# Four heads at a time in the decay weights of a chunked scan, and a ring of split activations in a pool of its own

## The chip, the cores and the metric

The kernel runs on one core of one Trainium2 chip. The metric is the device time of one execution in microseconds; lower is better. A core has TensorE (PE in the profile, with PEld for its weight loads), VectorE (DVE), ScalarE (ACT), GpSimd (POOL) and SyncE (SP), which issues the DMAs.

## The reference

One inference step of a hybrid backbone with 4 layers, 128 context tokens and 256 latent tokens, model width 1024. Layers 0 and 3 mix tokens by a bidirectional state-space scan (SSD), layer 1 by a short convolution, layer 2 by differential attention. Each is followed by a gated feed-forward network. The part that the change touches is the scan, here cut to its core for one direction (32 heads in 8 groups, chunks of 128 tokens):

```python
acs = jnp.cumsum(dtc * a, axis=2)
decay = jnp.exp(jnp.where(mask, acs[:, :, :, None] - acs[:, :, None], -jnp.inf))
cb = jnp.einsum('bcqgn,bcsgn->bcqsg', cc, bc)
y_diag = jnp.einsum('bcqsgr,bcsgrp->bcqgrp', cb[..., None] * decay * dtc[:, :, None], xf)
...
y = rmsnorm(y.reshape(bsz, L, SSM_D_INNER) * jax.nn.silu(z), norm_g)
return y @ w_out
```

It runs forwards and backwards, and both results are added.

## The kernel before

All 384 tokens are kept as three tiles of 128. Products with weights are made from float32r parts: a weight chunk is split into a high part (ScalarE, L155, `wh`) and a low part (VectorE, L156, `wl`), and three matmuls per block of 128 channels use hh, hl and wh, wl (L340 for channel-major blocks, L380 for the token-major output). The chunks stream from HBM through rings (`ahead`, L143). Modulation units (L187, `modps`) are put between the products by `pace`.

An SSD layer is `ssd` (L506). It opens a layer's pool `pl`, and inside it a core pool for the scan. `ssd_core` (L611) goes over 8 groups of four heads. While the scan of group g runs, the projections of group g + 1 are made (L340, then the convolution at L396 to L400), and the gate of group g (`sz`, L631). `scan` is a generator; its five steps are put between the projections. For each of the 3 chunks, `decay` (L674) builds the weights of the token pairs for the four heads:

- GpSimd: `e` = the backward difference for all four heads, 512 columns (L678), and `w` = C.B masked, times dt, backwards (L679).
- VectorE, once per head on 128 columns: `e` = min(forward difference, `e`) (L682).
- ScalarE: exp of `e` (L683).
- VectorE, once per head: `w` = C.B masked, times dt forwards, plus `w` (L686), then `w` times `e` for all heads (L687).

`e` and `w` share a ring of 4 buffers of 512 columns. For chunks 1 and 2 VectorE also makes `ab` (L693), the weights of the incoming states. The matmuls `yp` (L722) use them. The group ends with y (L741), the gate's product (L637), its square (L642) and the sum of squares `ssq` on GpSimd (L643).

After the groups, `ssq` goes through a matmul (`sps`, L523), and `tm_out` (L351) multiplies y by the output weights (L380): 16 steps of k, each with nine matmuls for a half of the columns. For each k, `prep` (L528) splits y into `yh` (ScalarE, L532) and `yl` (VectorE, L533). These lie in rings of RB = 7 buffers in the layer's pool `pl`.

The order on each engine is not the order of the code: the program is built with a scheduler that places instructions of the whole layer by a timeline of its own, and inserts waits. Buffers of a closed pool are given back tile by tile (`reuse_waits="tile"`), so a tile of a later pool waits for the last user of the space that it covers.

Of the kernel before, what the change touches and what calls it, by code (L numbers as in the profile page):

```python
# [10 lines left out]
F32 = mybir.dt.float32  # L11
F32R = mybir.dt.float32r
# [7 lines left out]
P = 128  # L20
# [24 lines left out]
class Net:  # L45
# [22 lines left out]
    @contextmanager  # L68
    def banked(self, **banks):
        """Five banks of PSUM, by what they are for."""  # L70
        with self.tc.tile_pool(name="ps", bufs=1, space=PSUM, reuse_waits="tile") as ps:
            self.ps, self.banks = ps, banks
            yield
# [46 lines left out]
    def plan(self, l):  # L120
        """The chunks of weights that layer l multiplies with, in their order."""
# [21 lines left out]
    def ahead(self):  # L143
        """Start the loads and the splits of the next chunks."""
# [14 lines left out]
    def weights(self, n):  # L159
        """The next chunk, [128, n], as two float32r parts whose sum it is; those after it are on their way."""  # L160
        self.ahead()
        assert self.wplan[self.wpos][1] == n
        self.wpos += 1
        return self.parts[self.wpos - 1]

# [1 line left out]
    def mod_units(self, l):  # L167
        """Closures that compute layer l's modulation; a unit is a megabyte of w_mod."""
# [56 lines left out]
    def modbuf(self):  # L225
        """A buffer for a unit of w_mod: the standing ones, or one of those that a phase has room for."""
# [15 lines left out]
    def pace(self, phase, n, of):  # L242
        """Modulation beside the products of a phase, n parts of which are done."""
# [15 lines left out]
    def sums(self, src):  # L259
        """Row sums of the squares of half a row, over D."""  # L260
# [5 lines left out]
    def rstd(self, sa, sb, eps=EPS):  # L266
        """(sa + sb + eps) ** -0.5"""
# [11 lines left out]
    def normed(self, t, ss):  # L279
        """The rows of token tile t, normed."""  # L280
# [7 lines left out]
    def turned(self, xn, banks=0):  # L288
        """Channel-major: two banks of [128 channels, 4 blocks, 128 tokens]."""
# [8 lines left out]
    def modulated(self, l, which, t, trs):  # L298
        """h's columns of token tile t, in two float32r parts."""
# [14 lines left out]
    def gated(self, t, hf, acc, gt, parts):  # L314
        """Half a token tile of m: its squares' sum and its product with the gate."""
# [5 lines left out]
    def residual(self, t, parts, eps=EPS):  # L321
        """x += gate * rmsnorm(m) * g for token tile t; the new rows' sums of squares."""
# [8 lines left out]
    def cm_block(self, chunks, nblk, b, m=P, tag="mm"):  # L331
        """[m channels, tokens] of h @ W; chunks: (first kb, number, hi, lo) as [128, kb, nblk, m]."""
# [18 lines left out]
    def tm_out(self, *args, room, **kw):  # L351
        """m = g @ W token-major, both halves, then the residual of each token tile."""
# [40 lines left out]
    def conv(self, src, cw):  # L393
        """Depthwise convolution of three taps along the tokens of both groups."""
# [113 lines left out]
    def ssd(self, l, pl, then):  # L508
# [11 lines left out]
        # eps over the square of the rows' norm factor, which is left out of y  # L520
# [7 lines left out]
        def prep(k):  # L528
            hi = pl.tile([P, T], F32R, tag="yh", name="yh", bufs=RB)
            lo = pl.tile([P, T], F32R, tag="yl", name="yl", bufs=RB)  # L530
            g = dn[:, k // 2, k % 2, 1:2]
            S.activation(hi, y[k], AF.Copy, scale=g)  # L532
            V.scalar_tensor_tensor(lo, y[k], g, hi.bitcast(F32), op0=ALU.mult, op1=ALU.subtract)  # L533
            return hi, lo

        self.tm_out(l, 0, 16, prep, eps=eps, then=then, room=1)

    def steps(self, j, keep, pl, between):
        """Time steps and decays: dt, the cumulated a*dt (token-major, and by rows in DRAM), and what states need."""
# [20 lines left out]
        # log1p(u) = 2 atanh(z), z = u / (2 + u) <= 1/3  # L560
# [17 lines left out]
        # cumulated within a chunk, forwards and backwards: rows of heads  # L578
# [15 lines left out]
        # what is left of a step at its chunk's end (for states), and a whole chunk's decay  # L594
# [16 lines left out]
    def ssd_core(self, l, j, keep, cw, dn, y, ssq):  # L611
# [3 lines left out]
        def convs(g, pr, out, tag="mm"):  # L615
            """Two blocks of channels after their convolution and SiLU, channel-major: (B, C) or (x, x)."""
# [28 lines left out]
        def scan(g, blocks):  # L645
# [11 lines left out]
            # token-major copies  # L657
# [14 lines left out]
            tt = lambda nm: pl.tile([P, 512], F32, tag="e", name=nm, bufs=4)  # L672

            def decay(t):  # L674
                # per head and pair of tokens: C.B, the decay of the direction in which it is one, and dt
                per = lambda a, dr: a[:, t, dr * 32 + 4 * g:dr * 32 + 4 * g + 4, None].to_broadcast([P, 4, P])
                e, w = tt("e"), tt("w")
                GP.tensor_tensor(h4(e), h4(abs_[t][:, 1]), per(acs, 1), op=ALU.subtract)  # L678
                GP.tensor_tensor(h4(w), cb[:, 1, t, None, :].to_broadcast([P, 4, P]), per(dt, 1), op=ALU.mult)  # L679
                for h in range(4):  # L680
                    hs, sl = 4 * g + h, slice(h * P, (h + 1) * P)
                    V.scalar_tensor_tensor(e[:, sl], abs_[t][:, 0, sl], acs[:, t, hs:hs + 1], e[:, sl], op0=ALU.subtract, op1=ALU.min)  # L682
                S.activation(e, e, AF.Exp)  # L683
                for h in range(4):
                    hs, sl = 4 * g + h, slice(h * P, (h + 1) * P)
                    V.scalar_tensor_tensor(w[:, sl], cb[:, 0, t, :], dt[:, t, hs:hs + 1], w[:, sl], op0=ALU.mult, op1=ALU.add)  # L686
# [333 lines left out]
```

## Time and profile before

| what | value |
|---|---|
| median of three runs | 2426.16 us (2422.03 to 2428.34) |
| span of the profiled execution | 2425.7 us, 35610 instructions |
| PE busy | 2298.7 us (95%) |
| DVE busy | 1647.8 us (68%) |
| ACT busy | 1225.8 us (51%) |
| POOL busy | 378.5 us (16%) |
| mean granted TensorE clock | 0.974 |

The page gives the profiled execution's span and no other time of its own; the runs of the first row were timed apart. Busy times are unions of an engine's instructions; the scan stages are about 93 to 390 us (layer 0) and 1790 to 2080 us (layer 3) of the span.

### The profile page before, as it was taken

To read this page: it belongs to the slowest core of one execution; us is meant where nothing else is said; L and a number is where in the kernel's file an instruction comes from. 1 tells how busy PE (TensorE), PEld (TensorE's weight loads), DVE (VectorE), ACT (ScalarE), POOL (GpSimd) and SP (SyncE) were. 2 spreads that over 40 slices of the span, in tenths; PEclk is the share of its full clock that TensorE was granted. 3 is DMA by queue.
4 is the path that set the end of the run, shared out by engine and by line. 5 is a ranking of instruction groups with operands and counts; after the bars stand their busy time and mean duration, and the time that the engine had idled before them with its cause. 6 is when DMAs were issued, how large, how long until landed. Compare 5 with 4: busy or idle time off the path is not lost.

```text
span 2425.7 us, 35610 instructions
## 1 busy us (share of the span) xinstructions
PE 2298.7 (95%) x13132; PEld 2007.5 (83%) x13132; DVE 1647.8 (68%) x2926; ACT 1225.8 (51%) x2031; POOL 378.5 (16%) x546
## 2 busy tenths in 40 slices
PE   6889999899999999999999989999998999989998
PEld 3778887599987978998688758998687888779987
DVE  3789877487755447776654547776669988677765
ACT  3646656454444344444544444445555766554444
POOL 1133330100001001000123330000114344010000
PEclk7989999999999999999999989999999999989999
DMA  7556565543547564335435453345455655423342
GB/s 285 173 164 194 171 202 191 200 137 122 165 120 268 212 215 162 130 122 165 148 116 178 164 205 128 123 131 163 138 171 174 194 160 162 133 97 122 126 146 85
DMA packets 113374, 391.79 MB, mean 162 GB/s; under 512 B 13104, under 2 KB 25520, under 8 KB 100912
## 3 DMA queue, kind: packets, MB, share of 16 engines
q1 hardware_dynamic: 113200, 389.52, 49.1%
q8 instruction: 103, 1.69, 0.3%
q14 instruction: 71, 0.58, 0.1%
HBM read 382.39 MB, written 7.08 MB: 161 GB/s over the span
## 4 chain that ended last, share of the span: by engine, by line
PE 76%; DVE 8%; DMA 3%; issue 2%; ACT 2%; POOL 2%; SPq 0%; POOLq 0%; DVEq 0%; ACTq 0%
PE mm L340 42%; PE mm L380 20%; PE mm L807 5%; PE modps L187 2%; PE yp L380 2%; DVE w L686 2%; DVE e L682 1%; DVE wl L156 1%; PE yp L848 1%; PE yp L722 1%; DMA wm<-in_w_mod 1%; DMA h<-in_state 1%; ACT jk L263 1%; DVE w L687 1%; POOL r L273 1%
## 5 line engine op out<-in xcount | busy, mean ns | idle before, releaser
L340 PE MATMUL mm<-hh,wh 128*128 128x384 f32 (+1 forms) x2352 | 798.0, 341 | 19.1 <-DVE cv L400 13.6
L340 PE MATMUL mm<-hl,wh 128*128 128x384 f32 (+1 forms) x2352 | 796.1, 339 | 0.0
L340 PE MATMUL mm<-hh,wl 128*128 128x384 f32 (+1 forms) x2352 | 792.1, 338 | 0.0
L156 DVE TENSOR_TENSOR wl<-wr,wh 128x1024 fp32r<-128x1024 f32 (+2 forms) x466 | 565.3, 1215 | 262.9 <-ACT wh L155 261.1
L155 ACT ACTIVATE wh<-wr 128x1024 fp32r<-128x1024 f32 (+2 forms) x466 | 483.2, 1039 | 328.0 <-PE mm L340 265.0
L340 PEld LDWEIGHTS mm<-hh,wh 128*128 128x128 f32 (+1 forms) x2352 | 444.3, 189 | 45.6 <-DVE cv L400 20.4
L340 PEld LDWEIGHTS mm<-hl,wh 128*128 128x128 f32 (+1 forms) x2352 | 443.9, 189 | 6.5 <-issue 4.2
L340 PEld LDWEIGHTS mm<-hh,wl 128*128 128x128 f32 (+1 forms) x2352 | 443.6, 189 | 2.6 <-issue 0.7
L396 ACT ACTIVATE cv<-mm,fcw 128x384 f32<-128x384 f32 x176 | 100.1, 571 | 233.2 <-PE mm L340 228.2
L380 PE MATMUL mm<-wh,gh 128*128 128x512 f32 x528 | 208.7, 395 | 0.0
L380 PE MATMUL mm<-wl,gh 128*128 128x512 f32 x528 | 208.6, 395 | 0.0
L380 PE MATMUL mm<-wh,gl 128*128 128x512 f32 x528 | 207.9, 395 | 0.0
L271 POOL TENSOR_SCALAR m<-s 128x1 f32<-128x1 f32 x42 | 17.6, 419 | 1146.7 <-ACT jk L263 1145.8
L398 DVE SCALAR_TENSOR_TENSOR cv<-mm,fcw,cv 128x127 f32<-128x127 f32 x352 | 144.1, 410 | 42.6 <-ACT cv L396 42.6
L405 ACT ACTIVATE gh<-fg 128x384 fp32r<-128x384 f32 x176 | 92.2, 524 | 152.6 <-PE mm L380 151.7
L406 DVE TENSOR_TENSOR gl<-fg,gh 128x384 fp32r<-128x384 f32 x176 | 97.6, 557 | 96.7 <-ACT gh L405 96.0
L400 DVE SCALAR_TENSOR_TENSOR cv<-mm,fcw,cv 128x127 f32<-128x127 f32 x352 | 145.8, 415 | 10.8
L380 PEld LDWEIGHTS mm<-wh,gh 128*128 128x128 f32 x528 | 99.0, 187 | 24.9 <-issue 0.8
L380 PEld LDWEIGHTS mm<-wh,gl 128*128 128x128 f32 x528 | 99.0, 187 | 24.3
L380 PEld LDWEIGHTS mm<-wl,gh 128*128 128x128 f32 x528 | 99.0, 187 | 23.9
L686 DVE SCALAR_TENSOR_TENSOR w<-cb,dt,w 128x128 f32<-128x128 f32 x192 | 94.8, 550 | 3.2 <-POOL w L679 3.2
L187 PE MATMUL modps<-wm,sil 128*32 128x512 f32 x496 | 81.8, 658 | 14.1 <-DMA wm<-in_w_mod 13.2
(223 smaller groups left out, 3206.2 us busy)
## 6 DMA issues: line engine op xcount, KB each, us to landing
wr<-in_ffn_up SPq DMA_DIRECT2D x176, 512.0 KB
wm<-in_w_mod SPq DMA_DIRECT2D x62, 1024.0 KB
wr<-in_ssd_in SPq DMA_DIRECT2D x96, 512.0 KB
wr<-in_ffn_down SPq DMA_DIRECT2D x88, 512.0 KB
wx<-in_w_mod SPq DMA_DIRECT2D x34, 1024.0 KB
ab<-acs SPq DMA_DIRECT2D x48, 512.0 KB
wr<-in_ssd_out SPq DMA_DIRECT2D x32, 512.0 KB
wr<-in_sc_in SPq DMA_DIRECT2D x32, 384.0 KB
```

The source lines that it names most:

```text
L155: self.S.activation(hi[:, :m], raw[:, :m], AF.Copy)
L156: self.V.tensor_tensor(lo[:, :m], raw[:, :m], hi[:, :m].bitcast(F32), op=ALU.subtract)
L187: self.PE.matmul(acc[32 * j:32 * j + 32, :], self.sil[:, kb, :], raws[:, j // 2, (j % 2) * 512:(j % 2 + 1) * 512], start=kb == 0, stop=kb ...
L340: self.PE.matmul(acc[:m], w, h, start=n == 0, stop=n == len(ops) - 1)
L380: self.PE.matmul(acc[t], g[:, o:o + n], w, start=k == 0 and i == 0, stop=k == nk - 1 and i == 2)
L396: self.S.activation(t, src, AF.Copy, scale=cw[:, 1:2])
L398: self.V.scalar_tensor_tensor(t[:, o + 1:o + n], src[:, o:o + n - 1], cw[:, 0:1], t[:, o + 1:o + n], op0=ALU.mult, op1=ALU.add)
L400: self.V.scalar_tensor_tensor(t[:, o:o + n - 1], src[:, o + 1:o + n], cw[:, 2:3], t[:, o:o + n - 1], op0=ALU.mult, op1=ALU.add)
L405: self.S.activation(hi, src, AF.Copy)
L406: self.V.tensor_sub(lo, src, hi.bitcast(F32))
L686: V.scalar_tensor_tensor(w[:, sl], cb[:, 0, t, :], dt[:, t, hs:hs + 1], w[:, sl], op0=ALU.mult, op1=ALU.add)
L807: PE.matmul(acc[t][:, :256], h[k][:, o:o + m], w[:, ws], start=k == 0 and i == 0, stop=k == KB - 1 and i == 2)
```

## The change

In `decay`, the eight VectorE instructions of 128 columns become three of 512 columns with broadcast operands (f, the minimum, the sum). The forward product with dt, which was fused into L686, becomes a GpSimd instruction with an output of its own, `u`. A chunk now takes four buffers of 512 columns, and their ring grows from 4 to 9. The rings of `yh` and `yl` leave the layer's pool for a pool that is opened after the core pool of the scan is closed. Comments and docstrings go as well; line numbers behind L527 shift by one, and inside `decay` differently (the new f is L682, minimum L684, `u` L686, sum L687, product L688 of the new file).

```diff
-        def prep(k):
-            hi = pl.tile([P, T], F32R, tag="yh", name="yh", bufs=RB)
-            lo = pl.tile([P, T], F32R, tag="yl", name="yl", bufs=RB)
...
-        self.tm_out(l, 0, 16, prep, eps=eps, then=then, room=1)
+        with self.tc.tile_pool(name=f"yhl{l}", bufs=1, reuse_waits="tile") as yp:
+            def prep(k):
+                hi = yp.tile([P, T], F32R, tag="yh", name="yh", bufs=RB)
+                lo = yp.tile([P, T], F32R, tag="yl", name="yl", bufs=RB)
...
+            self.tm_out(l, 0, 16, prep, eps=eps, then=then, room=1)
...
-            tt = lambda nm: pl.tile([P, 512], F32, tag="e", name=nm, bufs=4)
+            tt = lambda nm: pl.tile([P, 512], F32, tag="e", name=nm, bufs=9)
...
-                e, w = tt("e"), tt("w")
+                cbd = lambda i: cb[:, i, t, None, :].to_broadcast([P, 4, P])
+                e, f, w, u = tt("e"), tt("f"), tt("w"), tt("u")
                 GP.tensor_tensor(h4(e), h4(abs_[t][:, 1]), per(acs, 1), op=ALU.subtract)
-                GP.tensor_tensor(h4(w), cb[:, 1, t, None, :].to_broadcast([P, 4, P]), per(dt, 1), op=ALU.mult)
-                for h in range(4):
-                    hs, sl = 4 * g + h, slice(h * P, (h + 1) * P)
-                    V.scalar_tensor_tensor(e[:, sl], abs_[t][:, 0, sl], acs[:, t, hs:hs + 1], e[:, sl], op0=ALU.subtract, op1=ALU.min)
+                V.tensor_tensor(h4(f), h4(abs_[t][:, 0]), per(acs, 0), op=ALU.subtract)
+                GP.tensor_tensor(h4(w), cbd(1), per(dt, 1), op=ALU.mult)
+                V.tensor_tensor(e, f, e, op=ALU.min)
                 S.activation(e, e, AF.Exp)
-                for h in range(4):
-                    hs, sl = 4 * g + h, slice(h * P, (h + 1) * P)
-                    V.scalar_tensor_tensor(w[:, sl], cb[:, 0, t, :], dt[:, t, hs:hs + 1], w[:, sl], op0=ALU.mult, op1=ALU.add)
+                GP.tensor_tensor(h4(u), cbd(0), per(dt, 0), op=ALU.mult)
+                V.tensor_tensor(w, w, u, op=ALU.add)
                 V.tensor_tensor(w, w, e, op=ALU.mult)
```

The order on VectorE in the last scan group of layer 0, before, from the masked C.B (`cb`) on:

```order
L670 TENSOR_TENSOR cb<-cbp,trr 128x384 x2
L714 TENSOR_TENSOR s<-sp,s 128x256 x2
L686 SCALAR_TENSOR_TENSOR w<-cb,dt,w 128x128 x4
L682 SCALAR_TENSOR_TENSOR e<-ab,acs,e 128x128 x4
L687 TENSOR_TENSOR w<-w,e 128x512
L156 TENSOR_TENSOR wl<-wr,wh 128x1024
```

and at the same place now:

```order
L671 TENSOR_TENSOR cb<-cbp,trr 128x384 x2
L682 TENSOR_TENSOR f<-ab,acs 128x512
L715 TENSOR_TENSOR s<-sp,s 128x256 x2
L682 TENSOR_TENSOR f<-ab,acs 128x512
L687 TENSOR_TENSOR w<-w,u 128x512
L156 TENSOR_TENSOR wl<-wr,wh 128x1024
L688 TENSOR_TENSOR w<-w,e 128x512
L684 TENSOR_TENSOR e<-f,e 128x512
L694 TENSOR_TENSOR ab<-ab,cv 128x1024
```

The eight short instructions of a chunk are three long ones; the differences f stand ahead of the sums, and the first chunk's minimum has moved to before `cb`.

The order on TensorE at the end of the last projection of layer 0 (L340), before (`sp` is a chunk's state, `yp` the scan's output):

```order
L340 MATMUL mm<-hh_255,wl 128x384
L704 MATMUL sp<-xw,bt 128x256
L187 MATMUL modps<-wm,sil 32x512 x4
L380 MATMUL mm<-wh,yh 128x512
L380 MATMUL mm<-wl,yh 128x512
L380 MATMUL mm<-wh,yl 128x512
```

and now:

```order
L705 MATMUL sp<-xw,bt 128x256
L723 MATMUL yp<-w,xt 64x128 x4
L723 MATMUL yp<-ab,h_3238 64x128 x4
L723 MATMUL yp<-ab,s 64x128 x4
L187 MATMUL modps<-wm,sil 32x512 x4
L723 MATMUL yp<-w,xt 64x128 x4
L723 MATMUL yp<-ab,s 64x128 x4
L723 MATMUL yp<-ab,h_3240 64x128 x4
L201 MATMUL tp<-ident,brow 128x128 x4
L187 MATMUL modps<-wm,sil 32x512 x4
L523 MATMUL sps<-ones_126,ssq 128x1 x3
L380 MATMUL mm<-wh,yh 128x512
```

The output's products, which stood directly behind the projection and between the scan's, stand behind all of `yp` and behind the matmul on `ssq`. The first modulation unit with weights in the output's pool follows 15 of them later.

The order on ScalarE at the end of the scan of layer 0, before (`sq` is the square of the gated y):

```order
L691 ACTIVATE ab<-ab 128x1024
L532 ACTIVATE yh<-y_349,dn 128x384
L532 ACTIVATE yh<-y_350,dn 128x384
L710 ACTIVATE s<-sp 128x256
L155 ACTIVATE wh<-wr 128x1024
```

and now:

```order
L711 ACTIVATE s<-sp 128x256
L643 ACTIVATE sq<-y_356 128x384
L643 ACTIVATE sq<-y_357 128x384
L533 ACTIVATE yh<-y_342,dn 128x384
L533 ACTIVATE yh<-y_343,dn 128x384
L533 ACTIVATE yh<-y_344,dn 128x384
```

Before, `yh` of the eighth y (number 349) is made ahead of the scan's end; now that of the first y (342) comes behind the last squares.

## Rows read from the trace of the kernel before

**Rows 1.** The page: busy times, and the chain that ended last, by engine.
```profile
PE 2298.7 (95%) x13132; PEld 2007.5 (83%) x13132; DVE 1647.8 (68%) x2926; ACT 1225.8 (51%) x2031; POOL 378.5 (16%) x546
...
PE 76%; DVE 8%; DMA 3%; issue 2%; ACT 2%; POOL 2%; SPq 0%; POOLq 0%; DVEq 0%; ACTq 0%
```

**Rows 2.** Busy us by stretch: length, PE, PEld, DVE, ACT, POOL; clock, DMA, GB/s.
```profile
93.00:150.00 57.00, 42.27 (x270) 35.29 (x269) 50.45 (x97) 30.05 (x44) 24.62 (x27) 0.87 0.55 164
150.00:354.00 204.00, 196.57 (x1304) 175.27 (x1303) 169.54 (x315) 128.63 (x181) 73.97 (x75) 0.99 0.59 186
1796.00:1860.00 64.00, 54.59 (x348) 48.40 (x347) 51.48 (x100) 38.52 (x57) 26.15 (x26) 0.97 0.64 178
1860.00:2037.60 177.60, 171.69 (x1195) 156.93 (x1193) 160.87 (x311) 123.55 (x171) 73.31 (x72) 1.00 0.60 184
360.90:379.30 18.40, 18.01 (x124) 12.55 (x124) 18.20 (x33) 12.92 (x17) 3.18 (x2) 1.00 0.50 159
2052.60:2071.80 19.20, 18.58 (x120) 14.18 (x119) 19.09 (x36) 11.19 (x17) 2.25 (x3) 1.00 0.38 102
134.80:145.00 10.20, 5.51 (x40) 3.04 (x37) 10.20 (x24) 2.08 (x4) 3.08 (x3) 0.50 0.60 193
```

**Rows 3.** Waits of PE, 90 to 390 us (first two), 1770 to 2080 us.
```profile
PE yp L722 <- DVE w L687: 9.2, 5, 4.6
PE mm L340 <- DVE cv L400: 7.1, 5, 2.4
...
PE mm L340 <- DVE cv L400: 5.3, 8, 1.5
...
PE yp L722 <- DVE w L687: 4.2, 3, 2.0
```

**Rows 4.** Groups by line and shape: busy us, mean ns, idle before.
```profile
L682 DVE SCALAR_TENSOR_TENSOR e<-ab,acs,e 128x128 f32<-128x128 f32 x192 | 74.7, 442 | 1.3 <-POOL e L678 1.3
L686 DVE SCALAR_TENSOR_TENSOR w<-cb,dt,w 128x128 f32<-128x128 f32 x192 | 94.8, 550 | 3.2 <-POOL w L679 3.2
L687 DVE TENSOR_TENSOR w<-w,e 128x512 f32<-128x512 f32 x48 | 32.6, 678 | 0.1
L693 DVE TENSOR_TENSOR ab<-ab,cv 128x1024 f32<-128x1024 f32 x32 | 40.4, 1262 | 0.2 <-ACT ab L691 0.2
L156 DVE TENSOR_TENSOR wl<-wr,wh 128x1024 fp32r<-128x1024 f32 x432 | 533.9, 1237 | 252.4 <-ACT wh L155 250.7 <-DMA ab<-acs 0.8 <-DMA wr<-in_ssd_out 0.3
L679 POOL TENSOR_TENSOR w<-cb,dt 128x512 f32<-128x512 f32 x48 | 63.8, 1329 | 29.1 <-PE yp L722 15.1 <-DVE w L687 11.0 <-DVE cb L670 2.2
L637 DVE TENSOR_TENSOR y<-y,sz 128x384 f32<-128x384 f32 x32 | 21.9, 693 | 2.4 <-ACT sz L631 2.4
L643 POOL TENSOR_TENSOR ssq<-ssq,sq 128x384 f32<-128x384 f32 x30 | 33.0, 1099 | 62.9 <-ACT sq L642 62.7
```

**Rows 5.** By line and tile: ns min/median/max, first and last start (yh: 93 to 250 us).
```profile
L686 DVE SCALAR_TENSOR_TENSOR w<-cb,dt,w x192: 331/341/1137, 102.8 to 2063.8; 128x128 f32<-128x128 f32 x192
L679 POOL TENSOR_TENSOR w<-cb,dt x48: 1037/1085/3438, 101.7 to 2060.9; 128x512 f32<-128x512 f32 x48
...
L532 ACT ACTIVATE yh<-y,dn x7: 602/604/613, 128.4 to 233.2; 128x384 fp32r<-128x384 f32 x7
```

**Rows 6.** Timeline of DVE, last scan group of layers 0 and 3: start, us.
```profile
355.38 1.02 DVE L670 TENSOR_TENSOR cb<-cbp,trr 128x384 f32<-128x384 f32 x2 [3.60 <-PE cbp L667]
...
373.32 0.69 DVE L687 TENSOR_TENSOR w<-w,e 128x512 f32<-128x512 f32 x1
...
2047.92 1.02 DVE L670 TENSOR_TENSOR cb<-cbp,trr 128x384 f32<-128x384 f32 x2 [2.23 <-PE cbp L667]
```

**Rows 7.** The same stretches for L380 alone (PE and PEld columns only).
```profile
360.90:379.30 18.40, 12.00 (x48) 8.81 (x49) 1.00 0.50 159
2052.60:2071.80 19.20, 14.81 (x56) 10.34 (x57) 1.00 0.38 102
```

**Rows 8.** The chain in order of time, end of the scan of layer 0.
```profile
373.06 2.77 PE yp L722 x48
```

More of the change, by code (lines that the diff above doesn't have):

```diff
@@ L526, in ssd @@
         eps = [ep[:, t:t + 1] for t in range(NT)]
-        def prep(k):
-            hi = pl.tile([P, T], F32R, tag="yh", name="yh", bufs=RB)
-            lo = pl.tile([P, T], F32R, tag="yl", name="yl", bufs=RB)
[L531 to L534, printed above, removed]
-        self.tm_out(l, 0, 16, prep, eps=eps, then=then, room=1)
+        with self.tc.tile_pool(name=f"yhl{l}", bufs=1, reuse_waits="tile") as yp:
+            def prep(k):
+                hi = yp.tile([P, T], F32R, tag="yh", name="yh", bufs=RB)
+                lo = yp.tile([P, T], F32R, tag="yl", name="yl", bufs=RB)
+                g = dn[:, k // 2, k % 2, 1:2]
+                S.activation(hi, y[k], AF.Copy, scale=g)
+                V.scalar_tensor_tensor(lo, y[k], g, hi.bitcast(F32), op0=ALU.mult, op1=ALU.subtract)
+                return hi, lo
+            self.tm_out(l, 0, 16, prep, eps=eps, then=then, room=1)
     def steps(self, j, keep, pl, between):
```

## The prediction

> **What bounds the kernel now.** I read the page first, for the engine shares and the chain that ended last: TensorE is busy 95% of the span and carries 76% of the chain, while VectorE carries 8% [rows 1]. So the kernel is bound by TensorE, and work taken off VectorE shortens it only where TensorE stands still for VectorE. The change lies in layers 0 and 3 alone, so the second view is the table by stretch over these two stages [rows 2]. The reader should set TensorE's busy time against the length of each stretch: it is idle for 14.7 us of the first 57 (93 to 150 us, the scan's start in layer 0), for 9.4 of 64 at the start in layer 3, and for only 7.4 of 204 and 5.9 of 177.6 in the groups that follow. VectorE is busy 83 to 91% of the later stretches, so it is nearly a second bound. Third, the table of waits says which of TensorE's idle time ended with VectorE [rows 3]: 9.2 and 7.1 us in layer 0, 5.3 and 4.2 us in layer 3. These 25.8 us are the ceiling of what a lighter VectorE can give. Last come the groups of the scan's operations by line, with their means [rows 4], the spread of some of them [rows 5], and the end of the last scan group in both layers [rows 6 to 8], where the second half of the change acts.
>
> **The arithmetic on VectorE and GpSimd.** There are 48 calls of decay (3 chunks, 8 groups, 2 layers). Removed are 192 `e` instructions, 74.7 us busy, and 192 `w` instructions, 94.8 us, together 169.5 us [rows 4]. Added on VectorE are 3 x 48 instructions with 512 columns (the difference f, the minimum, the sum). The multiplication at L687 has that form and size: 32.6 us for 48. A broadcast operand costs nothing there: L693 has one and takes 1262 ns for 1024 columns, L156 has none and takes 1237 [rows 4]. So 97.8 us come in and VectorE loses 71.7 us, if nothing delays it.
>
> GpSimd gets a third product, 48 times, of the form of L679, at 1329 ns: 64 us more on an engine that is busy 378.5 us in all [rows 1, 4]. Its own time hides, but it hits VectorE: `w` has a median of 341 ns and a maximum of 1137, most of a GpSimd product (1037 at least) longer [rows 5]. Its mean, 550 ns, stands above that median by 209, and the mean of `e`, 442 ns for the same size, by 101 [rows 4]: 60 us over 2 x 192 instructions, or 0.62 us for each of the 96 products that run now. A third product of the same kind then costs VectorE 48 x 0.62 = 30 us. It may cost nothing (if it falls into VectorE's idle time) or 50 us (1.04 us each, the plain duration). So VectorE gets lighter by 42 us (22 to 72), 2.6 us in each of the 16 groups. The Trainium skill (SBUF — State Buffer, section "Who interferes with whom") says that a Vector instruction with two SBUF inputs and a GpSimd instruction that reads SBUF take turns, and that whoever starts first holds the shared port for the whole instruction. The trace agrees for single instructions (341 against 1137 ns); by the rule with every product met, the 30 us would be 50, my share of the gain 6 us in place of 12 and the sum 2448.
>
> The change also adds a wait: VectorE's sum w + u waits for GpSimd's u, the last of its three products. Behind the sum in VectorE's order stand a split of weights (wl), for which L340 waits, and the product with `e`, for which yp waits. A longer ring of scan tiles (9 in place of 4) lets `e` and f run a group ahead, so I take no cost beyond the delays above; were u late each time by its own 1.04 us, that is the same 50 us again.
>
> What of this reaches TensorE is at most the 25.8 us of [rows 3] and at least nothing. I take **12 us**, about half: 2.6 us a group is more than the 1.6 us a group that TensorE waits for VectorE, but the waits are set by which instruction stands in front, not by the sum, and at the start of layer 3 VectorE is busy only 51.5 of 64 us [rows 2], so something else ended part of that idle time.
>
> **The ring of split y.** Before, the buffers for yh and yl lie in the layer's pool, so the first seven parts are made during the scan (128 to 233 us for layer 0) [rows 5]. The first products of the output, L380, thus stand ready to fill TensorE while the last scan group runs on VectorE: 12.0 us of them by 379.3 us in layer 0, and 14.8 us by 2071.8 us in layer 3 [rows 7]. TensorE is busy 18.0 of 18.4 and 18.6 of 19.2 us there [rows 2]. After the change the ring takes space that the scan gives back. The rows of the order show what follows: every L380 comes behind the last scan product and behind the matmul on ssq, and every yh behind the two squares of the last y. TensorE has nothing to fill the last group with.
>
> How long it waits: from the first `cb` of the last group VectorE has `cb` (1.02 us), `s` (0.69, as L637, of nearly its size), two `ab` and two `wl` (5.0), and ten instructions of 512 columns (two f, two minima, three sums, three products; the minimum of the first chunk is done before), 10 x 0.68 [rows 4, 6]. That is 13.5 us if nothing delays it. Nine GpSimd instructions that delay it by 0.62 us each make it 19, by 1.04 us each 22.9. Before, the same stretch took 18.6 us in layer 0 (355.38 to 374.0) [rows 6]. I take 17.5. Then follow one chunk's yp 1.4 (half of the 2.77 for two) [rows 8], two y and two gates of the size of L637 2.8 and a sum on GpSimd 1.1 [rows 4], a square 0.6 (as one `yh`, [rows 5]), and 0.5 for the matmul on ssq and the hops: 6.4 us. So the first L380 starts 23.9 us after `cb`, at 379.3 us in layer 0 and 2071.8 in layer 3 on the old time axis [rows 6]. That is what [rows 7] count to.
>
> The loss is those 12.0 and 14.8 us, less what moves the other way into the gap. In layer 0 that is a modulation unit (1.0 us), a transpose and the ssq matmul, about 2.1 us. In layer 3 it is 1.6 us. So 9.9 + 13.2 = **23 us** lost. With 13.5 us for VectorE it is 15, with 22.9 it is 34. The seven yl per layer that leave the scan are not a gain of their own; they are inside the half that I credit above.
>
> **Two smaller terms.** In layer 0 a modulation unit whose weights land in a buffer of the output pool now stands 15 L380 behind the first. Its load waits for GpSimd to give the space back. 15 x 0.25 us [rows 7] is 3.8 us of cover for a megabyte, which takes 5.4 us at the 193 GB/s of a busy stretch [rows 2]: of the 1.6 that stick out I take **1 us**, with 0 to 4 as bounds. On SP's queue the later chunks of output weights now stand behind this load and the next of its kind; eight chunks of two k steps, 8 x 18 x 0.25 = 36 us of TensorE's work, are loaded ahead of them, so I cost that at nothing. Second, TensorE's clock. In the stretch 134.8 to 145 us it was granted at 0.50, the lower of its two levels, after a start in which it was idle for a quarter of the time; it was at 1.00 through both ends of the scan [rows 2]. With TensorE idle for about half of each gap, a drop like that one is likely: the 5.5 us busy in it would be 2.8 at full clock. **4 us** for both gaps, from 0 to 6.
>
> **Sum.** 2425.7 + 23 + 1 + 4 - 12 = 2441.7 us. The page gives no other time for its execution than the span. The median of the three runs, 2426.16, is 0.5 us above it, so I predict **2442 us**.
>
> **The rivals.** A: *the relief arrives whole.* All 25.8 us of waits go, the gap is at its shortest (15 us) and the clock holds: 2425.7 + 15 - 26 = 2415 us. It needs the third product to fall into idle time and the 512-column instructions to stay below about 0.72 us. For it speaks that VectorE carries the waits at the start of layer 0, the worst stretch [rows 2, 3]; against it, that delays by GpSimd are seen in the same instructions now [rows 5]. It decides from the point where the waits on VectorE give back more than the gap costs, some 23 us. I give it 0.20.
>
> B: *the two cancel.* Relief 20, gap 17, clock 3: 2426 us. For it speaks that relief and loss have the same size within their bounds; against it, that relief of 20 needs four fifths of all waits to go. 0.20.
>
> C: *GpSimd becomes a second bound through VectorE.* If each of the now 144 products delays a VectorE instruction for its whole 1.04 us, that is 150 us against 60 now: the 71.7 us saved are overspent by 18, the waits grow by some 10 us, and the gap costs 28 (between 23 and 34): 2425.7 + 10 + 28 = 2464 us. For it speaks the maximum of 1.14 us [rows 5]; against it, that the mean of L686 is half of that [rows 4]. I give it 0.15.
>
> The forecast itself (2430 to 2458) keeps 0.45.
>
> **How the numbers follow.** A measurement of this kernel can tell about 0.3%, 7 us, from no change. The forecast and C lie above that, 0.60. B is within it, 0.20. A is faster, 0.20. The bounds of the terms give 2415 (15 + 0 + 0 - 26) to 2470 (34 + 4 + 6 - 0). From 2416 to 2465 about half of A (0.10) and half of C (0.08) are left out.
>
> **What would show it.** In the profile after: the three new VectorE groups near 0.7 us each with 48, and GpSimd's `u` at 1.1 to 1.4; VectorE's total down by some 40 us; TensorE's waits on w and cv about halved; no yh or yl before the last scan product, and a stretch of some 18 us before the first L380 in each of the two layers in which TensorE is busy half the time. I am wrong if TensorE is busy there as now, if the first L380 comes less than 20 us after the last group's `cb`, or if VectorE's total falls by less than 20 us.

## The result, and the profile after

The changed kernel took **2507.4 us** (median of four runs, 2506.4 to 2508.7) where the kernel before took 2424.1 beside it: a ratio of 1.0339, 95% interval 1.0324 to 1.0353. That is 83 us slower; 16 were forecast (2442 against 2426.16), and the upper end of the range was 2465.

The page after, busy times and chain by engine, beside [rows 1]:

```profile
PE 2319.8 (93%) x13132; PEld 2030.0 (81%) x13132; DVE 1664.8 (66%) x2686; ACT 1232.5 (49%) x2033; POOL 480.6 (19%) x594
...
PE 73%; DVE 11%; DMA 7%; issue 3%; POOL 3%; ACT 2%; SPq 0%; POOLq 0%; ACTq 0%; DVEq 0%
```

VectorE did not get lighter by 42 us, it got heavier by 17 (1647.8 to 1664.8). GpSimd got busier by 102 us, for 48 more products of which each takes 1.03 us when alone.

Where the time went shows in the table by stretch (length; busy PE, PEld, DVE, ACT, POOL; clock, DMA, GB/s), cut at the scan's own marks: in each layer from the first C.B matmul (`cbp`) of the second group to that of the eighth, and, after the change, from there to the first L380. Before:

```profile
122.20:354.50 232.30, 216.10 (x1433) 190.30 (x1432) 196.40 (x368) 140.15 (x199) 85.80 (x88) 0.96 0.59 185
...
1838.20:2047.00 208.80, 200.48 (x1353) 181.53 (x1353) 187.56 (x360) 141.82 (x200) 89.70 (x88) 0.99 0.60 183
```

After:

```profile
122.60:366.60 244.00, 215.44 (x1411) 191.41 (x1410) 192.66 (x267) 142.77 (x197) 125.30 (x107) 0.97 0.55 178
366.60:395.90 29.30, 17.49 (x132) 12.66 (x131) 22.78 (x26) 13.29 (x19) 15.86 (x12) 0.82 0.49 174
...
1864.30:2105.40 241.10, 213.56 (x1367) 196.33 (x1366) 192.42 (x267) 139.24 (x195) 126.98 (x107) 0.93 0.51 161
2105.40:2135.60 30.20, 15.38 (x111) 12.85 (x111) 22.79 (x27) 10.92 (x17) 16.38 (x12) 0.73 0.28 83
```

Two things are to be seen. At the ends of the scans TensorE is busy for 17.5 of 29.3 and 15.4 of 30.2 us, as forecast. But the groups ahead of them, which were to get shorter, are longer by 12 and 32 us, and TensorE's idle time in them went from 16.2 to 28.6 us in layer 0 and from 8.3 to 27.5 in layer 3. In layer 3 that is 19 of the 32 us; the other 13 are TensorE's own busy time (200.5 to 213.6), at a granted clock of 0.93 where it was 0.99. TensorE's waits say for what it stood idle (90 to 400 us, then 1825 to 2140 us; us in total, times, longest), against 9.2 and 4.2 in [rows 3]:

```profile
PE yp L723 <- DVE w L688: 30.7, 15, 6.2
...
PE yp L723 <- DVE w L688: 24.4, 11, 3.6
```

These two stretches take in the ends of the scans. In the groups alone, as cut above, the same wait comes to 17.6 and 20.5 us; before, it was 7.2 in layer 0, and none in layer 3.

And VectorE's and GpSimd's groups by line (busy us, mean ns, idle before), beside [rows 4], say why:

```profile
L156 DVE TENSOR_TENSOR wl<-wr,wh 128x1024 fp32r<-128x1024 f32 x432 | 555.5, 1286 | 261.7 <-ACT wh L155 255.3 <-DMA wr<-in_ssd_in 5.8 <-DMA wr<-in_ssd_out 0.3
...
L687 DVE TENSOR_TENSOR w<-w,u 128x512 f32<-128x512 f32 x48 | 52.6, 1095 | 9.1 <-POOL u L686 9.1
L694 DVE TENSOR_TENSOR ab<-ab,cv 128x1024 f32<-128x1024 f32 x32 | 49.9, 1561 | 0.0
L684 DVE TENSOR_TENSOR e<-f,e 128x512 f32<-128x512 f32 x48 | 49.9, 1040 | 0.9 <-POOL e L681 0.9
...
L682 DVE TENSOR_TENSOR f<-ab,acs 128x512 f32<-128x512 f32 x48 | 46.7, 991 | 5.7 <-DMA ab<-acs 5.7
L688 DVE TENSOR_TENSOR w<-w,e 128x512 f32<-128x512 f32 x48 | 46.6, 972 | 0.2
...
L686 POOL TENSOR_TENSOR u<-cb,dt 128x512 f32<-128x512 f32 x48 | 75.9, 1581 | 0.0
L681 POOL TENSOR_TENSOR e<-ab,acs 128x512 f32<-128x512 f32 x48 | 72.1, 1503 | 96.3 <-issue 48.5 <-DVE wl L156 47.8
L683 POOL TENSOR_TENSOR w<-cb,dt 128x512 f32<-128x512 f32 x48 | 70.6, 1471 | 1.2 <-DVE cb L671 1.1
```

The new instructions were put at 0.68 us each; f, minimum and sum take 0.99 to 1.10 on the mean. The product at L688, which the change does not touch, went from 678 to 972 ns, and `wl` and `ab` grew too. The timelines of both engines in a middle group of layer 3 show how (start, us). VectorE:

```profile
1953.91 1.13 DVE L687 TENSOR_TENSOR w<-w,u 128x512 f32<-128x512 f32 x1
1954.96 2.06 DVE L156 TENSOR_TENSOR wl<-wr,wh 128x1024 fp32r<-128x1024 f32 x1
1956.94 1.53 DVE L688 TENSOR_TENSOR w<-w,e 128x512 f32<-128x512 f32 x1
1958.39 1.52 DVE L684 TENSOR_TENSOR e<-f,e 128x512 f32<-128x512 f32 x1
1959.83 2.06 DVE L156 TENSOR_TENSOR wl<-wr,wh 128x1024 fp32r<-128x1024 f32 x1
```

GpSimd at the same time:

```profile
1953.00 1.48 POOL L681 TENSOR_TENSOR e<-ab,acs 128x512 f32<-128x512 f32 x1
1954.45 1.48 POOL L683 TENSOR_TENSOR w<-cb,dt 128x512 f32<-128x512 f32 x1
1955.90 2.02 POOL L686 TENSOR_TENSOR u<-cb,dt 128x512 f32<-128x512 f32 x1
1957.88 1.48 POOL L681 TENSOR_TENSOR e<-ab,acs 128x512 f32<-128x512 f32 x1
1959.33 1.48 POOL L683 TENSOR_TENSOR w<-cb,dt 128x512 f32<-128x512 f32 x1
```

In this stretch the two engines take turns, one instruction each. Four of the five VectorE instructions are 0.85 us longer than alone (0.68 to 1.53, 1.21 to 2.06), the sum at L687 by 0.45, and each GpSimd product is longer by a part of what stands on VectorE (1.04 to 1.48 or 2.02). It is not so all the time: of the 192 instructions at L682, L684, L687 and L688, 87 took under 0.72 us, as if alone, and 56 took 1.4 us or more. On GpSimd it is the rule: 114 of its 144 products took more than 1.3 us, where before 79 of 96 stayed under 1.2. Before, its products did not run in such rows; their ring of 4 tiles made `e` wait 49.9 us for VectorE's product:

```profile
L678 POOL TENSOR_TENSOR e<-ab,acs 128x512 f32<-128x512 f32 x48 | 55.2, 1151 | 167.8 <-DMA ab<-acs 96.4 <-DVE w L687 49.9 <-ACT ab L691 12.6
```

In the changed kernel no such wait is left, and the products of three chunks follow each other. By the code that is the ring of 9; no run changes that ring alone.

### The profile page after: what moved, and what is told of

Same layout as the page of the kernel before. It is cut to its first block, busy times and chain, and to the rows that moved or that the text cites. A ratio compares the mean times of both kernels' runs of the same rounds, so it can differ in the third digit from the quotient of the medians.

```text
span 2504.6 us, 35324 instructions
## 1 busy us (share of the span) xinstructions
PE 2319.8 (93%) x13132; PEld 2030.0 (81%) x13132; DVE 1664.8 (66%) x2686; ACT 1232.5 (49%) x2033; POOL 480.6 (19%) x594
## 4 chain that ended last, share of the span: by engine, by line
PE 73%; DVE 11%; DMA 7%; issue 3%; POOL 3%; ACT 2%; SPq 0%; POOLq 0%; ACTq 0%; DVEq 0%
PE mm L340 40%; PE mm L380 19%; PE mm L808 4%; DMA wm<-in_w_mod 3%; PE modps L187 2%; DVE wl L156 2%; PE yp L380 2%; PE yp L723 2%; DVE w L687 1%; DVE ab L694 1%; DVE e L684 1%; DVE w L688 1%; PE yp L849 1%; DMA h<-in_state 1%; DVE f L682 1%
## 5 line engine op out<-in xcount | busy, mean ns | idle before, releaser
L340 PE MATMUL mm<-hh,wh 128*128 128x384 f32 (+1 forms) x2352 | 805.0, 344 | 15.0 <-DVE cv L400 7.7
L340 PE MATMUL mm<-hl,wh 128*128 128x384 f32 (+1 forms) x2352 | 799.3, 340 | 0.0
L340 PE MATMUL mm<-hh,wl 128*128 128x384 f32 (+1 forms) x2352 | 794.7, 339 | 0.0
L156 DVE TENSOR_TENSOR wl<-wr,wh 128x1024 fp32r<-128x1024 f32 (+2 forms) x466 | 587.0, 1261 | 271.8 <-ACT wh L155 265.2
L340 PEld LDWEIGHTS mm<-hh,wh 128*128 128x128 f32 (+1 forms) x2352 | 448.6, 191 | 38.7 <-issue 17.9
L340 PEld LDWEIGHTS mm<-hl,wh 128*128 128x128 f32 (+1 forms) x2352 | 447.7, 190 | 3.6 <-issue 1.4
L340 PEld LDWEIGHTS mm<-hh,wl 128*128 128x128 f32 (+1 forms) x2352 | 446.4, 190 | 5.1 <-issue 3.5
L380 PE MATMUL mm<-wh,gh 128*128 128x512 f32 x528 | 209.0, 396 | 0.0
L380 PE MATMUL mm<-wl,gh 128*128 128x512 f32 x528 | 208.7, 395 | 0.0
L380 PE MATMUL mm<-wh,gl 128*128 128x512 f32 x528 | 208.2, 395 | 0.0
L380 PEld LDWEIGHTS mm<-wh,gh 128*128 128x128 f32 x528 | 99.1, 188 | 25.4 <-issue 1.7
L380 PEld LDWEIGHTS mm<-wh,gl 128*128 128x128 f32 x528 | 99.1, 188 | 24.8 <-issue 0.8
L380 PEld LDWEIGHTS mm<-wl,gh 128*128 128x128 f32 x528 | 99.1, 188 | 23.9
L681 POOL TENSOR_TENSOR e<-ab,acs 128x512 f32<-128x512 f32 x48 | 72.1, 1503 | 96.3 <-issue 48.5
```

The source lines that it names most:

```text
L156: self.V.tensor_tensor(lo[:, :m], raw[:, :m], hi[:, :m].bitcast(F32), op=ALU.subtract)
L340: self.PE.matmul(acc[:m], w, h, start=n == 0, stop=n == len(ops) - 1)
L380: self.PE.matmul(acc[t], g[:, o:o + n], w, start=k == 0 and i == 0, stop=k == nk - 1 and i == 2)
```

## The experiments

After the result there were two theories. **L**: each GpSimd product delays VectorE, and VectorE's time in the scan reaches the end. **O**: any edit makes the scheduler order all engines anew, and a new order is worse than the one that the kernel before happens to have. To tell them apart, some kernels hold the order: a table of numbers lists each engine's instructions in the order of another kernel, and edges that only fix the order of issue, and wait for nothing, chain them.

```diff
         build(tc, d)
+        pin(tc)
...
+    for eng, tab in ORDER.items():
+        ins = [i for i in tc.nc.cur_bb.bb.instructions if str(i.engine).endswith("." + eng) and "PoolBoundary" not in type(i).__name__]
+        perm = np.cumsum(np.frombuffer(zlib.decompress(base64.b85decode(tab)), "<i2").astype(np.int64))
+        for a, b in zip(perm[:-1], perm[1:]):
+            tc.add_manual_dep(ins[b], ins[a].name, mybir.DependencyInfo(mybir.DependencyClass.NoSync, mybir.DependencyReason.DATA), reason="order")
```

All runs at a glance. The columns after the ratio are lengths in us in one profiled execution, worked out from the starts of `cbp` and L380: groups 2 to 7 of each layer, its end (from the eighth group's `cbp` to the layer's last L380), and the middle, from there to layer 3's first `cbp`.

| run | order | us more | ratio (95%) | groups L0 | end L0 | middle | groups L3 | end L3 |
|---|---|---|---|---|---|---|---|---|
| before | own | | | 232 | 88 | 1364 | 209 | 80 |
| changed | own | 83 | 1.0339 (1.0324-1.0353) | 244 | 101 | 1367 | 241 | 99 |
| e1_ring | own | 47 | 1.0205 (1.0181-1.0228) | 230 | 102 | 1375 | 219 | 94 |
| e2_arith | own | 79 | 1.0332 (1.0312-1.0352) | 252 | 92 | 1377 | 238 | 82 |
| e3_no_u | own | 84 | 1.0354 (1.0333-1.0376) | 257 | 100 | 1365 | 237 | 97 |
| e4_dup | own | 49 | 1.0205 (1.0189-1.0222) | 258 | 90 | 1364 | 236 | 79 |
| p1_dup | before's | 50 | 1.0203 (1.0178-1.0229) | 251 | 92 | 1364 | 223 | 82 |
| p2_order | e4_dup's | 19 | 1.0072 (1.0044-1.0100) | 242 | 89 | 1365 | 228 | 78 |
| p5_ring | before's | 31 | 1.0128 (1.0104-1.0152) | 230 | 102 | 1368 | 208 | 95 |
| p6_after | before's | 63 | 1.0261 (1.0233-1.0289) | 246 | 105 | 1367 | 220 | 97 |
| p3_e512 | before's | 43 | 1.0178 (1.0162-1.0193) | 237 | 102 | 1363 | 218 | 94 |
| p7_no_u | before's | 26 | 1.0102 (1.0085-1.0119) | 231 | 102 | 1366 | 209 | 95 |
| q1_no_u | changed's | 38 | 1.0155 (1.0130-1.0181) | 234 | 98 | 1364 | 220 | 98 |
| q2_rb4 | own | 36 | 1.0142 (1.0112-1.0172) | 230 | 90 | 1382 | 223 | 80 |
| c1_pin | before's | -19 | 0.9917 (0.9896-0.9939) | 228 | 92 | 1359 | 199 | 79 |
| c1_free | own | -11 | 0.9955 (0.9937-0.9973) | 225 | 88 | 1366 | 219 | 79 |

### One part at a time, in the scheduler's order

**e1_ring**: only the pool of the split y.

```diff
-            hi = pl.tile([P, T], F32R, tag="yh", name="yh", bufs=RB)
+                hi = yp.tile([P, T], F32R, tag="yh", name="yh", bufs=RB)
```

> The kernel before with the ring of split y alone moved to a pool of its own (old decay, ring of 4). Theory (the two halves of the change add up; the ends of the two scans cost 12.7 + 19.6 us of the 79 us that the changed kernel lost): +25 to +33 us, about 2452 us, with the groups before the last as long as before (232 and 209 us) and the first L380 some 22 to 30 us after the last group's cb. Rival (the ends are slow only because the new decay is slow there): +10 to +15 us, about 2437 us. Second rival (the ring is nearly everything, since the scan also loses its filler): +60 us or more.

47 us, above the first range. The ends cost 13 + 15 us, as in the changed kernel (13 + 20), with the old decay: so they come from the ring, and the rival falls. The other 20 us are in layer 3's groups and in the middle, where the edit changes no work. **e2_arith**: the new decay with the ring back in `pl`.

```diff
-            hi = pl.tile([P, T], F32R, tag="yh", name="yh", bufs=RB)
+            hi = pl.tile([P, T], F32R, tag="yh", name="yh", bufs=4)
```

> The changed kernel with the ring of split y back in the layer's pool; it needs 4 buffers there in place of 7 for the ring of 9 scan tiles to fit. Theory (the new decay itself slows the scan by 14 + 31 us, and the two halves add up): +40 to +52 us, about 2470 us. Rival (the new decay is harmless or a gain where the output's products can fill TensorE, the prediction's 12 us): 2415 to 2430 us.

79 us, far above 52: the ends are short again, the groups are longer by 20 and 29 us, and the middle by 12. The two halves alone (47 + 79) come to much more than both together (83). So each run holds something that belongs to neither half; e2_arith also has a shorter ring of split y than either kernel. **e3_no_u**: without the third product.

```diff
-                GP.tensor_tensor(h4(u), cbd(0), per(dt, 0), op=ALU.mult)
-                V.tensor_tensor(w, w, u, op=ALU.add)
+                V.tensor_tensor(w, w, w, op=ALU.add)
```

> The changed kernel without GpSimd's third product; the sum on VectorE reads w twice instead. The forward C.B product is left out. Theory A (the third product is what hurts: with it GpSimd and VectorE take turns for long stretches): 96 products as before, VectorE's excess over undisturbed durations falls from 107 to about 70 us, time 2440 to 2460 us. Theory B (the long 512-column forms and the order on VectorE hurt by themselves): 2485 us or more.

Theory A seemed to fall: no gain at all, although VectorE was busy for 34 us less than in the changed kernel. **e4_dup**: the kernel before with `w` made twice.

```diff
                 GP.tensor_tensor(h4(w), cb[:, 1, t, None, :].to_broadcast([P, 4, P]), per(dt, 1), op=ALU.mult)
+                GP.tensor_tensor(h4(w), cb[:, 1, t, None, :].to_broadcast([P, 4, P]), per(dt, 1), op=ALU.mult)
```

> The kernel before with GpSimd's product w made twice (48 more products of 1.04 us, same values). Theory A (each further product delays a VectorE instruction by about 0.8 us, 38 us in all, and the scan cannot take it): +20 to +40 us. Theory B (a third product is cheap beside short VectorE instructions): 0 to +8 us.

49 us: more than either theory. One run speaks for the products, one against, and neither can be trusted while the order moves with every edit.

### The order held

**p1_dup** is e4_dup in the order of the kernel before, **p2_order** the kernel before in the order of e4_dup: a crossed pair.

> The instructions of the run in which GpSimd makes the product w twice (49 us slower than before), but with the order of the kernel before on TensorE, VectorE, ScalarE and SyncE, written out as a table; GpSimd's 48 second products stand right behind the first. Theory O (what cost 49 us there was the order that the scheduler made anew, not the products): 0 to +8 us. Theory L (each GpSimd product delays VectorE and through it TensorE): +20 to +50 us.

> The instructions of the kernel before, unchanged, in the order of the run in which GpSimd makes w twice, as a table, without the second products. Theory O (order alone): +30 to +50 us, about 2466 us. Theory L (the products): within 8 us of the kernel before.

The product costs 50 us with not one other instruction moved: theory L. The order alone costs 19 us, between the two ranges: order counts too, but it is the smaller part. The two do not add: with the product, e4_dup's order (49 us) is no worse than that of the kernel before (50). So what an order costs hangs on the work that stands in it. The page of p1_dup, and VectorE's group of the sums on `w`:

```profile
PE 2307.2 (93%) x13132; PEld 2015.6 (82%) x13132; DVE 1677.2 (68%) x2926; ACT 1225.5 (50%) x2031; POOL 426.3 (17%) x594
...
L687 DVE SCALAR_TENSOR_TENSOR w<-cb,dt,w 128x128 f32<-128x128 f32 x192 | 129.0, 728 | 15.2 <-POOL w L680 15.2
```

VectorE is busy for 29.4 us more than before, and waits 15.2 us for GpSimd instead of 3.2: 41 us, of the 50 that the run is longer. What is added to VectorE in the scan reaches the end almost whole, though TensorE is the engine with 93%. (The rest was not traced; TensorE's own busy time is 8.5 us up as well.)

**p5_ring** is e1_ring, **p6_after** the changed kernel, with everything but the output's products of both layers in the order of the kernel before.

> The kernel before with the ring of split y in a pool of its own, and everything outside the output's products of the two layers held in the order of the kernel before by a table. The same edit cost 47 us with the scheduler's own order. Theory O (of these, 13 + 15 us are the two ends of the scans, the rest is new order elsewhere): +24 to +32 us, about 2453 us. Rival (the ring's move itself makes the groups and the later layers longer, by its buffers): +40 to +50 us.

> The changed kernel with the order of the kernel before, as a table: the new VectorE instructions stand where the first of the old eight stood, u stands behind w on GpSimd, and only the output's products of the two layers are free. Theory O: +24 to +35 us, all of it in the two ends (2450 to 2460 us), with scan groups of about 230 and 210 us. Theory L: the groups stay at 240 us and more and the time within 15 us of the changed kernel's, 2490 us or more.

p5_ring is at 31 us, all in the ends (14 + 16); 16 of e1_ring's 47 us were order. p6_after is between the theories: 32 us above p5_ring, most of it in the groups, with the order held, and 20 us below the changed kernel. These 20 us lie in layer 3's groups (220 us against 241): TensorE is busy there for 199.9 us at a granted clock of 1.00, in the changed kernel for 213.6 at 0.93.

**p7_no_u** leaves the third product out of p6_after (edit as in e3_no_u), **p3_e512** puts only f and the minimum into p5_ring; there f has one buffer of its own, and `e` and `w` keep their ring of 4.

```diff
+                f = pl.tile([P, 512], F32, tag="f", name="f")
+                V.tensor_tensor(h4(f), h4(abs_[t][:, 0]), per(acs, 0), op=ALU.subtract)
+                V.tensor_tensor(e, f, e, op=ALU.min)
-                for h in range(4):
-                    hs, sl = 4 * g + h, slice(h * P, (h + 1) * P)
-                    V.scalar_tensor_tensor(e[:, sl], abs_[t][:, 0, sl], acs[:, t, hs:hs + 1], e[:, sl], op0=ALU.subtract, op1=ALU.min)
```

> The changed kernel in the held order (2487 us) without GpSimd's third product; the sum reads w twice, so the forward C.B product is left out. Theory L: the 33 us go, VectorE's waits for GpSimd fall from 17.6 to about 3 us and its busy time by 20 to 35 us: 2445 to 2460 us. Theory W: 2475 us or more. (With the scheduler's own order the same omission gave nothing, 2510 us; if it gives nothing here either, the third product is not the cause in the new form.)

> The run with the ring alone and the held order (2455 us), and in it one part of the new arithmetic: the differences f and the minimum in single 512-column instructions; w and its two GpSimd products as before. Theory L (of the 33 us that the new arithmetic costs at a held order, the third GpSimd product and the wait for it are nearly all): 2448 to 2462 us. Theory W (the wide forms themselves cost it, since each stands longer in front of GpSimd and of VectorE's own queue): 2470 us or more.

Without the product 37 us go (63 to 26), and the groups are as short as before. The two pages and groups, p6_after first:

```profile
PE 2320.8 (93%) x13132; PEld 2019.6 (81%) x13132; DVE 1661.8 (67%) x2686; ACT 1229.0 (49%) x2031; POOL 471.0 (19%) x594
...
L687 DVE TENSOR_TENSOR w<-w,u 128x512 f32<-128x512 f32 x48 | 57.0, 1187 | 17.6 <-POOL u L686 17.6
```

```profile
PE 2311.2 (94%) x13132; PEld 2013.4 (82%) x13132; DVE 1634.9 (67%) x2686; ACT 1229.5 (50%) x2031; POOL 397.3 (16%) x546
...
L686 DVE TENSOR_TENSOR w<-w 128x512 f32<-128x512 f32 x48 | 53.3, 1110 | 5.4 <-POOL w L683 5.3
```

VectorE's busy time differs by 26.9 us and its wait for GpSimd by 12.3: 39 us for 37 in the time. p3_e512 came out 12 us above p5_ring, at 2469.7 us: 8 above theory L's range and at the edge of theory W's. So f and the minimum in place of four fused instructions cost some 12 us there, by their form or by f's one buffer; that was not told apart. With all of the wide forms (p7_no_u) the time is 5 us under p5_ring, and the intervals overlap, so that as a whole they neither cost nor give anything that these runs can tell.

**q1_no_u** leaves the product out in the changed kernel's own order; **q2_rb4** is the kernel before with 4 buffers for the split y (the edit shown at e2_arith) and a free order.

> The changed kernel without its third GpSimd product (the sum reads w twice, the forward C.B product is left out), in the changed kernel's own order as a table. With the scheduler's own order the omission gave 2510 us, in the order of the kernel before 2453 us, against 2487 us with the product. If the product costs the same in any order: 34 us less than the changed kernel, about 2472 us. If in the changed kernel's order something else holds the scan up: above 2490 us.

> The kernel before with 4 buffers in place of 7 for the split y, in the layer's pool, and nothing else; the scheduler makes its own order. If a new order costs by itself (17 to 19 us in the pairs so far): 2436 to 2450 us. If the order is no worse as long as the work is the same, and the smaller ring costs nothing: within 7 us of the kernel before.

In the changed kernel's order the product costs 45 us (83 to 38), 11 more than expected. e3_no_u gained nothing because its new order ate the gain: the same instructions are 58 us faster in the order of the kernel before, and 46 in the changed kernel's. q2_rb4 loses 36 us where no work changed, more than either range: 14 in layer 3's groups, 18 in the middle and 8 behind layer 3. Its ends, where the ring is used, are as short as before. But the loss is not an order's alone: e2_arith, the other run with four buffers, is also 8 us longer behind layer 3 and 12 in the middle, and no other run is more than 2 us longer behind layer 3. So the smaller ring has a share, through the layout or the order that it brings.

### A version that beats both

If GpSimd's products cost VectorE so much, fewer of them should pay. **c1_pin** and **c1_free** make `w` on ScalarE, in the held and in a free order:

```diff
-                GP.tensor_tensor(h4(w), cb[:, 1, t, None, :].to_broadcast([P, 4, P]), per(dt, 1), op=ALU.mult)
+                for h in range(4):
+                    hs, sl = 4 * g + h, slice(h * P, (h + 1) * P)
+                    S.activation(w[:, sl], cb[:, 1, t, :], AF.Copy, scale=dt[:, t, 32 + hs:32 + hs + 1])
```

> The kernel before with the backward product w made on ScalarE (four instructions of 128 columns, scaled by dt) in place of GpSimd, in the held order, the new instructions where GpSimd's product started. Theory L (VectorE's time in the scan, its delays by GpSimd included, reaches the end nearly one to one): the 41 us by which w's sums stand above their undisturbed time mostly go, 2390 to 2412 us. Rival (ScalarE, with some 65 us more, holds up the exponentials and the splits): 2426 to 2450 us.

> The same kernel as the last with the order that the scheduler makes. If a new order costs some 17 us as in the other runs: that much above the last, 2410 to 2430 us. If the scheduler's new order is sometimes as good as the one before: equal to the last.

c1_pin takes 2407.5 us, 0.8% less than the kernel before; c1_free 0.5% less, 9 us above c1_pin. The page of c1_pin, and VectorE's group:

```profile
PE 2294.2 (95%) x13132; PEld 2004.7 (83%) x13132; DVE 1611.8 (67%) x2926; ACT 1281.8 (53%) x2223; POOL 314.6 (13%) x498
...
L688 DVE SCALAR_TENSOR_TENSOR w<-cb,dt,w 128x128 f32<-128x128 f32 x192 | 73.4, 440 | 1.1 <-ACT w L681 1.1
```

VectorE loses 36 us without one instruction of its own removed: 21 at the sums on `w` (94.8 to 73.4 us, the mean from 550 to 440 ns), the rest at its neighbours. ScalarE takes 56 us more, and the kernel is shorter all the same. Of 36 us of relief 19 reach the end.

## Why the prediction was wrong, step by step

In steps that add up: the ring 31 us (p5_ring), the wide forms -5 (p7_no_u less p5_ring), the third product 37 (p6_after less p7_no_u), the new order 20 (changed less p6_after): 83. The last two depend on the way taken: over q1_no_u the order is 12 and the product 45.

- **The ring of split y** (23 + 1 + 4 = 28 us forecast): right. p5_ring lost 31, nearly all in the two ends. From `cb` to the first L380 23.9 us were worked out; layer 0 of p5_ring took 25.7 (352.03 to 377.7), the changed kernel 28.5 and 29.3. The granted clock fell as supposed: 0.82 and 0.73 in the two ends of the changed kernel, where TensorE was busy for 60% and 51% of the time; it was 1.00 before [rows 2]. What that fall cost, and the 1 us for the modulation unit, were not measured apart. That the clock would also fall in layer 3's groups (0.93) is in no term.
- **"VectorE loses 71.7 us, if nothing delays it"**: here the sum failed first. It took the old 169.5 us away whole, and put undisturbed durations (0.68) in their place. But 60 us of the old time were delays by GpSimd's `e` and `w`, as the same paragraph had it, and these two products stay: their delays moved onto f, the minimum, the sum, L688, `wl` and `ab`. Without the 60 us only 12 of the 71.7 are left. Undisturbed instructions in the timeline of the kernel before say the same (start, us):

```profile
361.00 1.13 DVE L682 SCALAR_TENSOR_TENSOR e<-ab,acs,e 128x128 f32<-128x128 f32 x4
362.05 0.68 DVE L687 TENSOR_TENSOR w<-w,e 128x512 f32<-128x512 f32 x1
362.65 1.21 DVE L156 TENSOR_TENSOR wl<-wr,wh 128x1024 fp32r<-128x1024 f32 x1
```

  Each starts a little before the one ahead of it has ended, so the time from start to start counts: four short ones hold VectorE for 1.05 us (361.00 to 362.05), a 512-column one for 0.60. Old, undisturbed: 2 x 1.05 a chunk; new: 3 x 0.60. That is 0.3 us a chunk, 14 us in 48, not 71.7. It was measured, too: p7_no_u, all wide and without the third product, has VectorE busy for 1634.9 us, 13 less than before and 8 less than p5_ring (1642.9). Those 14 off and some 30 on for the third product come to about the 17 by which VectorE got heavier.
- **The third product's delays** (30 us, "0.62 us for each"): right in size. VectorE's busy time rose by 26.9 us in the new form and 29.4 in the old one, 0.56 and 0.61 us for each product.
- **The wait for u** ("I take no cost beyond the delays above"): wrong. VectorE stood still 12 us more for it in both pairs with the held order of the kernel before.
- **"So VectorE gets lighter by 42 us", and half of the waits go, -12**: VectorE got 17 us heavier, and what was added came through about one to one (50 us for 41 in p1_dup, 37 for 39 in p6_after less p7_no_u, 45 for 36 in the changed kernel less q1_no_u, busy time and wait together). Relief came through at half in the one run that gives it (19 for 36 in c1_pin, where ScalarE got heavier as well). The sum had one price for both directions. The ceiling of 25.8 us bounds a gain only.
- **The order**: not in the sum at all. The rows of the order were read for the two ends, where they move by design; that the scheduler would set the order of the whole program anew was not costed. It is worth 20 us here, and in the other pairs -1 (e4_dup and p1_dup), 9 (c1), 12 (q1_no_u and p7_no_u), 16 (e1_ring and p5_ring), 19 (p2_order and the kernel before) and 58 (e3_no_u and p7_no_u). What in an order makes it good was not settled. The traces show one thing that an order changes: how often ScalarE loads a table for its functions (1.28 us each), 79 times in the kernel before, 81 in the changed one, 95 in e4_dup and p2_order. It does not decide alone, for c1_free has 71 such loads and c1_pin 79, and c1_pin is the faster.

Rival C had the mechanism, GpSimd as a second bound through VectorE, but a price of "its whole 1.04 us" for each product where 0.56 to 0.61 came, and its 2464 us lacked the wait for u and the order. Of the checks named beforehand, the new groups near 0.7 us (0.99 to 1.10), GpSimd's `u` at 1.1 to 1.4 (1.58), VectorE's total (down by 40; up by 17) and the halved waits failed; the gaps ahead of the first L380 were seen.

The Trainium skill (SBUF — State Buffer, section "Who interferes with whom") has the lock as exclusive, held by whoever started first. The timelines after agree in both directions, with up to 0.85 us on VectorE and 0.44 or 0.98 on GpSimd. The 2448 us that were worked out by it had the same two faults, the old delays taken away and no order.

## What to carry to other kernels

When a busy time holds delays by another engine's work, these delays don't leave with the instructions that show them: take the undisturbed time away (start to start, in a stretch where nothing interferes), and let the delays fall on what comes instead. Before a product is moved to GpSimd beside a VectorE that is 85% busy in its stage, ask whether ScalarE can take it: here one product more a chunk on GpSimd cost 37 to 50 us, and one fewer, made on ScalarE, gave 19. Where a scheduler sets the order, an edit's price is known only with the order held; without it one run here hid a gain of 46 to 58 us.

## What the hardware showed that was not expected

The price is per meeting, not per column. A VectorE instruction that meets a whole GpSimd product is longer by 0.80 to 0.85 us whether it has 128 columns (0.34 to 1.14), 512 (0.68 to 1.53) or 1024 (1.21 to 2.06), while the product waits for the VectorE instruction: 1.04 us become 1.48 beside 512 columns and 2.02 beside 1024, and stay at 1.07 to 1.18 on the mean beside short ones (p1_dup). VectorE pays about as much for each further product in either form (0.56 and 0.61 us). What the wide forms change is GpSimd's side: beside short instructions its products pass almost undelayed, beside wide ones they wait as well, so that of 102 us more on GpSimd only some 50 are the third product.
